# One-hots of an expert routing matrix made per token with tensor_scalar, and three rows of U h beside each block

## The chip, the cores and the metric

One core of a Trainium2 chip runs the whole kernel in one launch. The metric is the device time of an execution in microseconds; before the change three runs gave 2013.26, 2014.86 and 2017.14 us, a median of 2014.86.

## The reference

One layer over 512 latent tokens and 256 context tokens, width 1024: an input projection, two mixers (neighbourhood attention and a recurrence), an output projection, and then the part that matters here, an expert layer with 16384 experts. For each token, 8 heads score 128 + 128 sub-keys, take the best 16 of each side, add all pairs, and keep the best 16 sums. Each kept pair names an expert (i, j):

```
idx = take_along_axis(i1 * 128 + i2, pos)         # 8 heads x 16 experts per token
g   = softmax(top)
a   = gelu(einsum('tpkd,td->tpk', u[idx], t))
out = einsum('tpk,tpkd->td', g * a, v[idx])
```

A gated residual and a final RMSNorm follow.

## The kernel before, in words

The kernel does not gather the experts of the first 384 tokens. It computes the activations of all 16384 experts for these tokens as dense products, and multiplies them by a matrix W that holds the gate weight of each (expert, token) and is zero where the expert was not chosen. Only the last 128 tokens gather their rows of u and v by indirect DMA (`gathered`). Both ways run together.

The expert layer (`experts`) has these stages:

- Retrieval: queries, scores, and the search for the best 16 (`Retrieval.run`, `rank`). Beside it, `steps(RSTEPS)` issues three rows of U h after each of seven heads. One row (`Activations.step`) is 128 experts against 384 tokens: a load of u, a split into a rounded part (ScalarE, uhi) and a rest (GpSimd, ulo, line 69), 24 products of 384 columns (lines 396, 397, 399), and a gelu (line 400). The first seven pairs of rows stay in SBUF, later ones are written to DRAM and read back in the V stage.
- Routing: for each group of 128 tokens `slots` turns the expert numbers into two halves, transposes them on TensorE and copies them to eT (the two halves) and gw (the gate weight as a high and a low f16 part). Then twelve blocks of 32 tokens (`Routing.block`) build W. For one token, W is a 128 x 128 matrix: the product of the one-hot matrix of the second half (128 slots on the partitions, 128 values) with the one-hot matrix of the first half times the gate. VectorE makes four tokens at a time with two tensor_tensor operations (lines 348 and 351), laid out so that the token is the innermost index; TensorE does two products per token (line 356), ScalarE evicts four tokens (line 357), and one DMA per block writes 2 MB of W. Ahead of each block, `steps(WSTEPS)` issues two rows of U h.
- V stage: 128 iterations c, each with 18 products of 512 columns of a row of V against W times the activations (line 555). Rows of U h that are still missing are issued here, one per iteration, as soon as `up.n < c + 16`. The gathers of the last 128 tokens are issued between: per group of four iterations nine of them, or three while the rows of U h are ahead (`GRATE`, line 527). There are 259 gather iterations (128 rows of u, 128 of v, and a lag of 3); what is left after the loop runs behind it (line 567). Then `finish` normalises and writes the output.

The order of instructions on each engine is made by the framework's planner from the program order and its own estimates of durations, so rows of U h are interleaved with routing products; gathers and the operations on their rows are pinned to program order. Buffers (three hot, three hg, two stage, three uhi and ulo) bound how far an engine runs ahead. W must be in DRAM before the V stage's first loads.

Of the kernel before, what the change touches and what calls it, by code (L numbers as in the profile page):

```python
# [22 lines left out]
F32 = mybir.dt.float32  # L23
F32R = mybir.dt.float32r
F16 = mybir.dt.float16
U32 = mybir.dt.uint32
I32 = mybir.dt.int32
AF = mybir.ActivationFunctionType
ALU = mybir.AluOpType
# [3 lines left out]
P = 128  # L33
# [10 lines left out]
PH, NK, TOPK = 8, 128, 16  # L44
# [50 lines left out]
def layer(ctx: ExitStack, tc: tile.TileContext, a: dict):  # L95
# [49 lines left out]
    output_projection(tc, a, ident, ones, modx, s2x, mix, h2, hg, xnat)  # L145
    right.close()
    experts(tc, ctx, a, dram, ident, modx, h2, hg, xnat)


# [7 lines left out]
GSCALE = 2.0 ** 14  # L157
# [3 lines left out]
TD = ND * P  # L161


class Retrieval:
# [3 lines left out]
    def __init__(self, tc, ctx, a):  # L168
        nc = self.nc = tc.nc
        self.tc, self.a = tc, a  # L170
        self.pool = lambda c, name, bufs, **kw: c.enter_context(tc.tile_pool(name=name, bufs=bufs, reuse_waits="tile", **kw))
        one = self.pool(ctx, "r1", 1)
        self.top = one.tile([P, NT, PH, TOPK], F32, name="top")
        self.ex = one.tile([P, NT, PH, TOPK], F32, name="ex")
# [132 lines left out]
    def slots(self, m, wk, ps, ident, eT, gw):  # L307


        nc = self.nc  # L310
        flat = lambda t: t[:, m].rearrange("p h k -> p (h k)")
        sl = slice(m * P, (m + 1) * P)
        eu, ru = (wk.tile([P, P], U32, name=n) for n in ("eu", "ru"))
        rc = wk.tile([P, 2, P], F32, name="rc")
        nc.vector.tensor_copy(out=eu, in_=flat(self.ex))
        t = ps.tile([P, 3, P], F32, name="et", bufs=1)
        for i, (op, imm) in enumerate(((ALU.logical_shift_right, 7), (ALU.bitwise_and, NK - 1))):
            nc.vector.tensor_scalar(out=ru, in0=eu, scalar1=imm, scalar2=None, op0=op)
            nc.vector.tensor_copy(out=rc[:, i], in_=ru)
            nc.tensor.transpose(out=t[:, i], in_=rc[:, i], identity=ident)  # L320
        nc.tensor.transpose(out=t[:, 2], in_=flat(self.top), identity=ident)
        nc.scalar.activation(out=eT[:, :, sl], in_=t[:, 0:2], func=AF.Copy)
        nc.scalar.activation(out=gw[:, 0, sl], in_=t[:, 2], func=AF.Copy, scale=GSCALE)
        nc.vector.scalar_tensor_tensor(out=gw[:, 1, sl], in0=t[:, 2], scalar=GSCALE, in1=gw[:, 0, sl], op0=ALU.mult, op1=ALU.subtract)


class Routing:

    NB = 4

    def __init__(self, tc, ctx, a, ps, eT, g, W):
        nc = self.nc = tc.nc
        pool = lambda name, bufs, **kw: ctx.enter_context(tc.tile_pool(name=name, bufs=bufs, reuse_waits="tile", **kw))
        self.wk, self.st, self.ps = pool("wwk", 3), pool("wst", 2), ps
        self.eT, self.g, self.W = eT, g, W
        raw = self.st.tile([P, NK, WBLK], F32, name="stage").rearrange("p i t -> p (i t)")[:, 0:NK]
        nc.scalar.dma_start(out=raw, in_=a["iota"])
        self.iota = self.wk.tile([P, NK, self.NB], F16, name="iota16", bufs=1)
        nc.vector.tensor_copy(out=self.iota, in_=raw[:, :, None].to_broadcast([P, NK, self.NB]))

    def block(self, b):
        nc, NB = self.nc, self.NB
        stage = self.st.tile([P, NK, WBLK], F32, name="stage")
        for g in range(WBLK // NB):
            at = b * WBLK + g * NB
            shape = [P, 2, NK, NB]
            hot = self.wk.tile(shape, F16, name="hot")
            nc.vector.tensor_tensor(out=hot, in0=self.iota[:, None].to_broadcast(shape),
                                    in1=self.eT[:, :, None, at:at + NB].to_broadcast(shape), op=ALU.is_equal)
            hg = self.wk.tile(shape, F16, name="hg")  # L350
            nc.vector.tensor_tensor(out=hg, in0=hot[:, 0:1].to_broadcast(shape),
                                    in1=self.g[:, :, None, at:at + NB].to_broadcast(shape), op=ALU.mult)
            o = self.ps.tile([P, NB, NK], F32, name="wo")
            for t in range(NB):
                for i in range(2):
                    nc.tensor.matmul(out=o[:, t], lhsT=hot[:, 1, :, t], rhs=hg[:, i, :, t], start=(i == 0), stop=(i == 1))  # L356
            nc.scalar.activation(out=stage[:, :, g * NB:(g + 1) * NB].rearrange("p i t -> p t i"), in_=o, func=AF.Copy,
                                 scale=1.0 / GSCALE)
        nc.sync.dma_start(out=self.W[:, :, b].rearrange("g j x -> j g x"), in_=stage.rearrange("j (g i) t -> j g (i t)", i=GRP))
# [92 lines left out]
LASTV = ((0, 0), (0, 8), (2, 0), (2, 8))  # L452
WQB = 8
AHEAD, UBUFS = 9, 3
RSTEPS, WSTEPS = 3, 2
GRATE = (9, 3)


def experts(tc, ctx, a, dram, ident, modx, h2, hg, xnat):
    nc = tc.nc  # L460
# [14 lines left out]
    def steps(n):  # L475
        for _ in range(n):
            up.step()

    with ExitStack() as c2:
        c2.enter_context(tc.using_default_side("right"))  # L480
        ret = Retrieval(tc, c2, a)
        ret.run(h2, lambda: steps(RSTEPS))
        for g in range(2):
            sl = hg[:, g * 512:(g + 1) * 512]
            t = ups.tile([P, 4, P], F32, name="ut")
            for k in range(4):
                nc.tensor.transpose(out=t[:, k], in_=sl[:, k * P:(k + 1) * P], identity=ident)
            nc.scalar.activation(out=sl, in_=t.rearrange("p k d -> p (k d)"), func=AF.Copy)
        one = pool(c2, "w1", 1)
        eT = one.tile([P, 2, TD], F16, name="eT")  # L490
        gw = one.tile([P, 2, TD], F16, name="gw")
        ps = pool(c2, "wps", 2, space=PSUM)
        rt = Routing(tc, c2, a, ps, eT, gw, W)
        ret.softmax(one)
        for m in range(ND):
            ret.slots(m, one, ps, ident, eT, gw)
        nc.vector.tensor_copy(out=idx, in_=ret.ex[:, ND].rearrange("p h k -> p (h k)"))
        nc.gpsimd.tensor_copy(out=weight, in_=ret.top[:, ND].rearrange("p h k -> p (h k)"))
        for b in range(TD // WBLK):
            steps(WSTEPS)  # L500
            rt.block(b)
        steps(up.n % 2)
# [4 lines left out]
    with ExitStack() as c2:  # L507
# [14 lines left out]
        for c in range(NK):  # L522
            g, i = divmod(c, GRP)
# [4 lines left out]
            if i % 2 == 0:  # L528
                q = c // 2
                up.fetch(q + AHEAD)  # L530
                raw = vp.tile([P, 2, D], F32, name="vraw")
# [18 lines left out]
            for m in range(ND):  # L550
                sl = slice(m * P, (m + 1) * P)
                for r, vh, vl in vs:
                    for x, y in ((wh, vh), (wh, vl), (wl, vh)):
                        for d in range(2):
                            nc.tensor.matmul(out=acc[m][:, d * 512:(d + 1) * 512], lhsT=x[:, r, sl], rhs=y[:, d * 512:(d + 1) * 512],  # L555
                                             start=(c == 0 and y is vh and x is wh),
                                             stop=(last and r == 1 and x is wl))
# [41 lines left out]
class Weights:  # L599
# [22 lines left out]
    def col(self, ct):  # L622
        pieces = self.pieces
        return lambda k: tuple(t[:, k % 2, ct * P:(ct + 1) * P] for t in pieces[k // 2])
# [604 lines left out]
```

## Time and profile before

| what | value |
|---|---|
| profiled execution | 2013.56 us |
| its span | 2011.8 us |
| median of three runs | 2014.86 us |
| TensorE busy | 1832.2 us, 91% |
| VectorE busy | 1443.1 us, 72% |
| GpSimd busy | 954.2 us, 47% |
| ScalarE busy | 760.7 us, 38% |

Busy time is the time in which an engine has an instruction in it; matmuls are pipelined, so their durations overlap and the distance between starts is what one costs. The profile names instructions by line and by the tiles that they write and read (`out<-in`), with partitions x elements and type. In the timeline several equal instructions in a row are merged: the duration then runs from the first start to the last end. "PEld" is the loading of weights on TensorE. The profiled execution's time is 1.8 us over its span.

### The profile page before, as it was taken

To read this page: it belongs to the slowest core of one execution; us is meant where nothing else is said; L and a number is where in the kernel's file an instruction comes from. 1 tells how busy PE (TensorE), PEld (TensorE's weight loads), DVE (VectorE), ACT (ScalarE), POOL (GpSimd) and SP (SyncE) were. 2 spreads that over 40 slices of the span, in tenths; PEclk is the share of its full clock that TensorE was granted. 3 is DMA by queue.
4 is the path that set the end of the run, shared out by engine and by line. 5 is a ranking of instruction groups with operands and counts; after the bars stand their busy time and mean duration, and the time that the engine had idled before them with its cause. 6 is when DMAs were issued, how large, how long until landed. Compare 5 with 4: busy or idle time off the path is not lost.

```text
span 2011.8 us, 25393 instructions
## 1 busy us (share of the span) xinstructions
PE 1832.2 (91%) x9501; PEld 1578.0 (78%) x9501; DVE 1443.1 (72%) x2407; ACT 760.7 (38%) x1074; POOL 954.2 (47%) x651
## 2 busy tenths in 40 slices
PE   8999996998899999789988999999999999999870
PEld 4787875776777888688886889999999898888650
DVE  6625385668646799988856677777767777777877
ACT  5322243444435333267653333333333333333311
POOL 2411013333015355622215557767676777677663
PEclk8999997999998999999998999999999999999985
DMA  7317531000134333257778878878787878787885
GB/s 273 100 48 249 190 108 44 9 17 9 48 126 157 109 111 121 86 164 213 225 231 326 335 277 288 304 277 301 269 305 283 299 282 297 279 301 274 333 277 193
DMA packets 140506, 409.11 MB, mean 203 GB/s; under 512 B 11488, under 2 KB 62048, under 8 KB 123488
## 3 DMA queue, kind: packets, MB, share of 16 engines
q1 hardware_dynamic: 93440, 244.20, 34.3%
q0 software_dynamic: 42336, 153.24, 21.9%
q10 hardware_dynamic: 4608, 10.06, 1.3%
q8 instruction: 74, 1.21, 0.2%
q14 instruction: 48, 0.39, 0.1%
HBM read 370.76 MB, written 36.70 MB: 203 GB/s over the span
## 4 chain that ended last, share of the span: by engine, by line
PE 56%; DVE 15%; DMA 14%; issue 9%; POOL 4%; ACT 2%; SPq 0%; POOLq 0%; DVEq 0%; ACTq 0%
PE acc L555 17%; DMA rows<-v,gidx 10%; PE ua L399 6%; PE ua L397 5%; PE ua L396 5%; PE wo L356 3%; PE pj L78 2%; PE pj L77 2%; PE G L817 2%; PE pj L76 2%; DVE gacc L434 2%; POOL rows L417 1%; PE G L881 1%; DVE qk L810 1%; PE qp L78 1%
## 5 line engine op out<-in xcount | busy, mean ns | idle before, releaser
L396 PE MATMUL ua<-h,uhi 128*128 128x384 f32 x1024 | 347.1, 339 | 0.9 <-ACT act L400 0.9
L397 PE MATMUL ua<-h,uhi 128*128 128x384 f32 x1024 | 345.2, 337 | 0.0
L69 POOL TENSOR_TENSOR ulo<-uraw,uhi 128x1024 fp32r<-128x1024 f32 x87 | 213.6, 2458 | 207.4 <-PE ua L399 82.3
L422 DVE CUSTOM_DVE_ANT_0 rows<-rows,hg 128x1024 f32<-128x1024 f32 x128 | 200.0, 1576 | 99.2 <-DMA rows<-u,gidx 99.2
L434 DVE SCALAR_TENSOR_TENSOR gacc<-rows,dots,gacc 128x1024 f32<-128x1024 f32 x127 | 202.4, 1594 | 95.3 <-DMA rows<-v,gidx 93.8
L555 PE MATMUL acc<-vhi,wh 128*128 128x512 f32 x768 | 240.8, 395 | 14.0 <-ACT vhi L66 14.0
L555 PE MATMUL acc<-vlo,wh 128*128 128x512 f32 x768 | 240.5, 394 | 13.7 <-DVE vlo L69 13.7
L66 ACT ACTIVATE uhi<-uraw 128x1024 fp32r<-128x1024 f32 x128 | 135.8, 1062 | 283.4 <-DMA uraw<-uT 168.1
L555 PE MATMUL acc<-vhi,wl 128*128 128x512 f32 x768 | 239.6, 393 | 0.0
L417 POOL DMA_INDIRECT rows<-u,gidx x128 | 200.2, 1564 | 73.2 <-DVE dots L422 51.5
L417 POOL DMA_INDIRECT rows<-v,gidx x128 | 193.7, 1514 | 84.1 <-DVE gacc L434 55.1
L535 POOL TENSOR_TENSOR w<-w,act 128x768 f32<-128x768 f32 x64 | 145.2, 2287 | 144.5 <-DMA w<-W 139.6
L399 PE MATMUL ua<-h,ulo 128*128 128x384 f32 x1024 | 204.7, 338 | 2.8 <-POOL ulo L69 2.8
L396 PEld LDWEIGHTS ua<-h,uhi 128*128 128x128 f32 x1024 | 193.8, 189 | 5.1 <-ACT act L400 1.5
L397 PEld LDWEIGHTS ua<-h,uhi 128*128 128x128 f32 x1024 | 193.5, 189 | 4.2
L66 ACT ACTIVATE vhi<-vraw 128x1024 fp32r<-128x1024 f32 x128 | 134.6, 1054 | 149.8 <-PE acc L555 132.4
L69 DVE TENSOR_TENSOR vlo<-vraw,vhi 128x1024 fp32r<-128x1024 f32 x128 | 170.2, 1332 | 28.6 <-ACT vhi L66 28.6
L555 PEld LDWEIGHTS acc<-vlo,wh 128*128 128x128 f32 x768 | 144.9, 190 | 49.1 <-DVE vlo L69 17.3
L399 PEld LDWEIGHTS ua<-h,ulo 128*128 128x128 f32 x1024 | 179.0, 188 | 5.1 <-POOL ulo L69 5.0
L555 PEld LDWEIGHTS acc<-vhi,wh 128*128 128x128 f32 x768 | 144.4, 189 | 39.4 <-ACT vhi L66 14.3
L555 PEld LDWEIGHTS acc<-vhi,wl 128*128 128x128 f32 x768 | 145.4, 189 | 31.5
L618 DVE TENSOR_TENSOR wlo<-raw,whi 128x1024 fp32r<-128x1024 f32 (+1 forms) x68 | 80.1, 1196 | 93.4 <-ACT whi L615 92.9
(339 smaller groups left out, 3359.1 us busy)
## 6 DMA issues: line engine op xcount, KB each, us to landing
uraw<-uT SPq DMA_DIRECT2D x64, 1024.0 KB
vraw<-vP SPq DMA_DIRECT2D x64, 1024.0 KB
W<-stage SPq DMA_DIRECT2D x12, 2048.0 KB
w<-W SPq DMA_DIRECT2D x32, 768.0 KB
raw<-w_in SPq DMA_DIRECT2D x32, 512.0 KB
sg<-wmB POOLq DMA_DIRECT2D x21, 512.0 KB
raw<-wq SPq DMA_DIRECT2D x32, 256.0 KB
act<-act ACTq DMA_DIRECT2D x16, 384.0 KB
```

The source lines that it names most:

```text
L66: nc.scalar.activation(out=hi, in_=src, func=AF.Copy)
L69: (lo_eng or nc.vector).tensor_tensor(out=lo, in0=src, in1=hi.bitcast(F32), op=ALU.subtract)
L78: nc.tensor.matmul(out=out, lhsT=ll, rhs=rh, start=False, stop=stop and k == n - 1)
L396: nc.tensor.matmul(out=o, lhsT=hi[:, k], rhs=hh[:, k], start=(k == 0), stop=False)
L397: nc.tensor.matmul(out=o, lhsT=hi[:, k], rhs=hl[:, k], start=False, stop=False)
L399: nc.tensor.matmul(out=o, lhsT=lo[:, k], rhs=hh[:, k], start=False, stop=(k == KT - 1))
L417: tc.keep_in_program_order(nc.gpsimd.indirect_dma_start(out=t[:], out_offset=None, in_=a[src], in_offset=bass.IndirectOffsetOnAxis(ap=idx[ ...
L422: tc.keep_in_program_order(nc.vector.tensor_tensor_reduce(out=t, in0=t, in1=h, op0=ALU.mult, op1=ALU.add, scale=1.0, scalar=0.0, accum_out ...
L434: tc.keep_in_program_order(nc.vector.scalar_tensor_tensor(out=acc, in0=t, scalar=dots[:, s:s + 1], in1=acc, op0=ALU.mult, op1=ALU.add))
L535: nc.gpsimd.tensor_tensor(out=wp, in0=wp, op=ALU.mult, in1=rows(up.done[q]))
L555: nc.tensor.matmul(out=acc[m][:, d * 512:(d + 1) * 512], lhsT=x[:, r, sl], rhs=y[:, d * 512:(d + 1) * 512], start=(c == 0 and y is vh and ...
L618: lo_eng.tensor_tensor(out=lo, in0=raw, in1=hi.bitcast(F32), op=ALU.subtract)
```

## The change

The one-hots are made token by token: one tensor_scalar compares the list 0..127 with the token's second half (a scalar on each partition), and two more compare it with the first half and multiply by the high or the low part of the gate. hot and hg then hold each token's 128 values side by side. [...] And WSTEPS goes from 2 to 3.

```diff
@@ Retrieval.slots
+        g16 = wk.tile([P, P], F16, name="g16")
...
-        nc.scalar.activation(out=gw[:, 0, sl], in_=t[:, 2], func=AF.Copy, scale=GSCALE)
+        nc.scalar.activation(out=g16, in_=t[:, 2], func=AF.Copy, scale=GSCALE)
+        nc.vector.tensor_copy(out=gw[:, 0, sl], in_=g16)
@@ Routing.__init__
-        self.iota = self.wk.tile([P, NK, self.NB], F16, name="iota16", bufs=1)
-        nc.vector.tensor_copy(out=self.iota, in_=raw[:, :, None].to_broadcast([P, NK, self.NB]))
+        self.iota = self.wk.tile([P, NK], F16, name="iota16", bufs=1)
+        nc.vector.tensor_copy(out=self.iota, in_=raw)
@@ Routing.block
-            shape = [P, 2, NK, NB]
-            hot = self.wk.tile(shape, F16, name="hot")
-            nc.vector.tensor_tensor(out=hot, in0=self.iota[:, None].to_broadcast(shape),
-                                    in1=self.eT[:, :, None, at:at + NB].to_broadcast(shape), op=ALU.is_equal)
-            hg = self.wk.tile(shape, F16, name="hg")
-            nc.vector.tensor_tensor(out=hg, in0=hot[:, 0:1].to_broadcast(shape),
-                                    in1=self.g[:, :, None, at:at + NB].to_broadcast(shape), op=ALU.mult)
+            hot = self.wk.tile([P, NB, NK], F16, name="hot")
+            hg = self.wk.tile([P, NB, 2, NK], F16, name="hg")
+            for t in range(NB):
+                col = lambda x, i: x[:, i, at + t:at + t + 1]
+                nc.vector.tensor_scalar(out=hot[:, t], in0=self.iota, scalar1=col(self.eT, 1), scalar2=None, op0=ALU.is_equal)
+                for i in range(2):
+                    nc.vector.tensor_scalar(out=hg[:, t, i], in0=self.iota, scalar1=col(self.eT, 0), scalar2=col(self.g, i),
+                                            op0=ALU.is_equal, op1=ALU.mult)
...
-                    nc.tensor.matmul(out=o[:, t], lhsT=hot[:, 1, :, t], rhs=hg[:, i, :, t], start=(i == 0), stop=(i == 1))
+                    nc.tensor.matmul(out=o[:, t], lhsT=hot[:, t], rhs=hg[:, t, i], start=(i == 0), stop=(i == 1))
@@
-RSTEPS, WSTEPS = 3, 2
+RSTEPS, WSTEPS = 3, 3
@@ experts
-        eT = one.tile([P, 2, TD], F16, name="eT")
-        gw = one.tile([P, 2, TD], F16, name="gw")
+        eT = one.tile([P, 2, TD], F32, name="eT")
+        gw = one.tile([P, 2, TD], F32, name="gw")
```

## Rows read from the trace of the kernel before

**Rows 1.** The page: busy time of each engine; granted clock in 40 slices.

```profile
PE 1832.2 (91%) x9501; PEld 1578.0 (78%) x9501; DVE 1443.1 (72%) x2407; ACT 760.7 (38%) x1074; POOL 954.2 (47%) x651
PEclk8999997999998999999998999999999999999985
```

**Rows 2.** Table of stretches: us, busy (instructions) per engine, clock, DMA share, GB/s.

```profile
860.60:1042.30 181.70, 174.85 (x1225) 160.64 (x1224) 152.48 (x204) 128.28 (x139) 43.86 (x17) 1.00 0.68 206
...
1066.50:1207.00 140.50, 140.50 (x617) 116.72 (x618) 98.63 (x100) 49.86 (x53) 79.01 (x45) 0.99 0.82 310
1207.00:1867.80 660.80, 657.98 (x3321) 595.77 (x3320) 495.92 (x443) 225.59 (x277) 472.74 (x261) 1.00 0.79 288
1867.80:1949.00 81.20, 67.52 (x278) 53.46 (x277) 63.52 (x49) 20.19 (x21) 52.08 (x34) 0.96 0.87 317
1949.00:1991.80 42.80, 2.64 (x12) 1.86 (x10) 28.66 (x23) 0.00 (x0) 23.61 (x20) 0.56 0.76 258
```

**Rows 3.** Groups, 860.6 to 1042.3: count, busy us, mean ns, idle before.

```profile
L357 ACT ACTIVATE stage<-wo 128x512 f32<-128x512 f32 x96 | 103.1, 1123 | 41.5 <-PE wo L356 41.3
L356 PE MATMUL wo<-hg,hot 128*128 128x128 f16 x768 | 102.7, 296 | 6.6 <-DVE hg L351 6.2
L348 DVE TENSOR_TENSOR hot<-iota,eT 128x1024 f16<-128x1024 f16 x96 | 84.2, 885 | 25.5 <-PE wo L356 24.9 <-ACT eT L322 0.4
L356 PEld LDWEIGHTS <-hot 128*128 128x128 f16 x768 | 81.7, 118 | 20.3 <-DVE hg L351 11.8 <-issue 5.1 <-DVE gw L324 0.2
L351 DVE TENSOR_TENSOR hg<-hot,gw 128x1024 f16<-128x1024 f16 x96 | 73.0, 798 | 0.0
...
L69 POOL TENSOR_TENSOR ulo<-uraw,uhi 128x1024 fp32r<-128x1024 f32 x17 | 43.9, 2580 | 129.6 <-PE ua L399 58.6 <-ACT stage L357 41.8 <-ACT uhi L66 20.1
...
L396 PEld LDWEIGHTS ua<-h,uhi 128*128 128x128 f32 x149 | 29.1, 195 | 0.1
L66 ACT ACTIVATE uhi<-uraw 128x1024 fp32r<-128x1024 f32 x19 | 20.4, 1074 | 10.3 <-PE ua L397 10.2
```

**Rows 4.** Gelus of U h rows ended before routing, and in it (line 400).

```profile
L400 ACT ACTIVATE act<-ua x27: 467/490/494, 639.9 to 855.9; 128x384 f32<-128x384 f32 x27
...
L400 ACT ACTIVATE act<-ua x19: 492/540/566, 867.3 to 1042.1; 128x384 f32<-128x384 f32 x19
```

**Rows 5.** TensorE timeline (start us, us) and line 219's durations.

```profile
1017.35 2.05 PE L356 MATMUL wo<-hg,hot 128*128 128x128 f16 x16 [0.21 <-DVE hg L351]
...
1019.41 0.34 PE L397 MATMUL ua<-h,uhi 128*128 128x384 f32 x1
1019.58 0.34 PE L396 MATMUL ua<-h,uhi 128*128 128x384 f32 x1
1019.76 0.35 PE L397 MATMUL ua<-h,uhi 128*128 128x384 f32 x1
...
536.12 0.61 PE L881 MATMUL G<-npT,vnac 128*128 128x128 f32 x4
...
L219 PE MATMUL sp<-keys,q x128: 270/275/377, 631.0 to 816.2; 128*128 128x128 f32 x128
```

**Rows 6.** VectorE tensor_tensor by line: count, minimum/median/maximum ns, first and last start.

```profile
L348 DVE TENSOR_TENSOR hot<-iota,eT x96: 676/686/2906, 860.6 to 1036.9; 128x1024 f16<-128x1024 f16 x96
L351 DVE TENSOR_TENSOR hg<-hot,gw x96: 676/684/2901, 861.5 to 1037.6; 128x1024 f16<-128x1024 f16 x96
L281 DVE TENSOR_TENSOR hot<-at_near,posf x16: 302/319/2430, 698.9 to 849.5; 128x320 f16<-128x320 f16 x16
L281 DVE TENSOR_TENSOR hot<-at_all,posf x16: 555/564/673, 699.3 to 849.7; 128x800 f16<-128x800 f16 x16
...
L305 DVE TENSOR_TENSOR top<-top,sm x1: 691/691/691, 855.6 to 855.6; 128x512 f32<-128x512 f32 x1
...
L585 DVE TENSOR_TENSOR tsq<-acc,gate x3: 1214/1214/1218, 1993.0 to 1997.8; 128x1024 f32<-128x1024 f32 x3
```

**Rows 7.** VectorE with scalars: durations by line, then timeline (start us, us).

```profile
L431 DVE TENSOR_SCALAR gacc<-rows,dots x1: 753/753/753, 1583.3 to 1583.3; 128x1024 f32<-128x1024 f32 x1
...
L872 DVE TENSOR_SCALAR np<-np,nz x32: 449/486/489, 325.0 to 549.6; 128x512 f32<-128x512 f32 x32
...
L752 DVE SCALAR_TENSOR_TENSOR state<-state,dec,G x4: 341/341/348, 355.6 to 356.3; 128x128 f32<-128x128 f32 x4
...
355.55 1.12 DVE L752 SCALAR_TENSOR_TENSOR state<-state,dec,G 128x128 f32<-128x128 f32 x4 [3.94 <-PE G L745]
...
419.48 0.49 DVE L872 TENSOR_SCALAR np<-np,nz 128x512 f32<-128x512 f32 x1
419.88 0.42 DVE L820 COPY_PREDICATED amat<-masks,G 128x256 f32<-128x256 uint32 x1
...
2001.49 0.21 DVE L593 TENSOR_SCALAR tt<-tt 128x1 f32<-128x1 f32 x2
2001.61 0.14 DVE L588 TENSOR_SCALAR tv<-tv 128x1 f32<-128x1 f32 x1
```

**Rows 8.** Timeline of GpSimd and VectorE at 856; durations of line 319.

```profile
856.12 2.35 POOL L69 TENSOR_TENSOR ulo<-uraw,uhi 128x1024 fp32r<-128x1024 f32 x1 [1.39 <-ACT uhi L66]
856.19 2.36 DVE L319 CAST rc<-ru 128x128 f32<-128x128 uint32 x1
...
L319 DVE CAST rc<-ru x6: 219/224/2361, 856.2 to 865.8; 128x128 f32<-128x128 uint32 x6
```

**Rows 9.** The gathered rows' additions behind 1949 (line 434).

```profile
L434 DVE SCALAR_TENSOR_TENSOR gacc<-rows,dots,gacc x23: 1283/1285/1348, 1948.1 to 1990.5; 128x1024 f32<-128x1024 f32 x23
```

## The prediction

> **What bounds the kernel now.** I read the busy shares and slices of the page first, then a table of stretches, then the groups, waits and instruction spacings inside the one stretch that the change touches, then the end of the kernel. TensorE is busy for 91% of the span and is granted most of its clock [rows 1], but its stages have different limits. [...]
>
> TensorE's terms in routing: sixteen token products run in 2.05 us, so one starts every (2.05 - 0.30)/15 = 0.117 us; 768 of them make 89.8 us [rows 5]. A row of U h (24 products of 384 columns, started every 0.1725 us [rows 5]) makes 4.14 us; 27 rows end before the stage and 19 in it [rows 4], so 78.7 us. Together 168.5, and 13.2 us of the stage is neither.
>
> **The change, part by part.**
>
> *Products.* Same 768, now with contiguous operands. Their cost lies between 0.117 us as now and a third of a 384-column product, 0.0575 us: 89.8 or 44.2 us. The nearest row is a 128-column f32 product with contiguous moving rows, (0.61 - 0.275)/3 = 0.112 us [rows 5]; f16 weights load in 0.118 us where f32 ones take 0.195 [rows 3], so f16 may do better. I take 0.09 us, 69 us; under the forecast it lies beneath VectorE and does not enter the sum.
>
> [...]
>
> *One-hots.* Removed: 96 + 96 tensor_tensor of 1024 f16. They occupy 84.2 + 73.0 = 157.2 us [rows 3], of which 96 x (0.686 + 0.684) = 131.5 is their own [rows 6] and 25.7 is waiting behind the 17 GpSimd subtractions of ulo, 1.5 us for each; the longest one-hot took 2.906, that is 2.22 us more than its own [rows 6]. Added: three tensor_scalar of 128 f16 per token, 1152 in all, with one or two scalars read per partition. No row has this form, so I build it from its parts.
> - Data: f32 tensor_tensor runs (1.214 - 0.691)/512 = 1.02 ns an element, f16 tensor_tensor (0.564 - 0.319)/480 = 0.51, f32 tensor_scalar (0.753 - 0.486)/512 = 0.52 [rows 6, 7]. If f16 halves a tensor_scalar as it halves a tensor_tensor, 128 elements cost 0.033 us; if not, 0.067.
> - Fixed: four instructions of 128 f32 elements with a per-partition scalar (L752) take 1.12 us, each 0.341, so one starts every 0.260 us; less 0.131 of data leaves 0.129. L872 (512 f32, such a scalar too) is followed 0.40 us later by the next instruction, less 0.266 leaves 0.134. Without such a scalar two one-element tensor_scalar start 0.07 apart (0.21 for both, 0.14 for one) [rows 7]. So the fetched scalar costs about 0.06 us that the next instruction does not hide.
> - Sum: 0.129 + 0.033 = 0.162 us, 1152 times, 186.6 us. Low end 0.07 + 0.033 = 0.103 (fetch hidden): 119 us. High end 0.260, as L752 stands: 300 us. I take 0.162, since L872 is the nearest row in kind (tensor_scalar, both sides in SBUF) and agrees with L752 on the fixed part.
>
> [...]
>
> *GpSimd's ulo.* A single-source instruction is held by it as well: a 128-element cast that takes 0.224 us took 2.36 beside a subtraction that began 0.07 us before it [rows 8]. So each subtraction in the stage holds VectorE for up to 2.22 us. There were 17; with one more row in each of 12 blocks there are 29. At 1.5 us each 44, at 2.2 us 64. Now that VectorE is seldom idle I take 64.
>
> *VectorE in routing:* 186.6 + 64 + 3 (the slots of the other two token groups, and the added copy of g16) + 2 (last product and eviction) = 255.6 us. TensorE needs 69 to 89.8 + 31 x 4.14 = 128.3 + 13.2 = 211 to 231 us and is hidden beneath it; ScalarE needs 103 us of evictions and 1.07 + 0.54 us a row [rows 3, 4], 153 in all. The hot and hg tiles have three buffers, so VectorE runs up to 12 tokens ahead, and products queue on TensorE in order behind whichever one-hot is late. The stage grows by 255.6 - 181.7 = 74 us.
>
> *Rows moved.* Twelve rows leave the V stage: 12 x 4.14 = 49.7 us of TensorE there. But the pace of gathers follows up.n: a group of four rows of V issues three while the rows of U h are ahead of it and nine while they are not. With up.n = 46 at the start the groups at c = 0 to 28 issue three: 8 x 3 + 24 x 9 = 240 of 259 iterations in the loop, 19 behind it. With 58 eleven groups do: 33 + 189 = 222, and 37 behind it. The tail runs one per (1990.5 - 1948.1)/22 = 1.93 us [rows 9], so it grows by 18 x 1.93 = 34.7 us. Net in the V stage: -15 us. The moved rows' transfers (6 loads of 1 MB through SP, 6 more pairs of act written through ScalarE's queue and read back) add 8.4 MB to a stage that moves 206 x 181.7 = 37.4 MB [rows 2] and gets longer: hidden. The 2.4 MB read back fall where the DMA share is 0.82; uncovered they would cost 2.4/0.31 = 8 us.
>
> **Sum.** +74 - 15 = +59 us. The profiled execution took 2013.56 us (span 2011.8); 2072.5. The median of the runs is 1.3 us above it: 2074.
>
> **Rivals.**
> 1. *The one-hots cost more.* The second scalar costs another 0.06 us (768 instructions, +46), or f16 does not halve the data time (1152 x 0.034 = +39): about 2115. For: no row has two scalars or f16 here. Against: both might be fetched together.
> 2. *TensorE stays the bound, products as slow as now.* VectorE under 231 us (the fixed part at about 0.10, or subtractions that hold it 1.5 us): 231 - 181.7 - 15 = +35, 2049. [...]
> 3. *Faster.* Products start every 0.0575 us: 44.2 + 128.3 + 13.2 = 186 us; +4 - 15 = -11, 2004. It decides on VectorE: it must be done in 186 us, so one instruction in (186 - 5 - 44)/1152 = 0.119 us, between the spacing without a fetched scalar (0.103) and the one with it (0.162). For: L593's 0.07. Against: L752 and L872. [...]
> 4. Between 2 and 3: quick products, one-hots at 0.13 us: VectorE 150 + 50 + 5 = 205; +23 - 15, 2023.
> [...]
>
> **Chances.** Forecast (2055 to 2095) 0.50; rival 1 0.17; rival 2 0.11; rival 3 0.13; rival 4 0.05; rival 5 0.04. The range reaches from just above rival 3 to just above rival 1. Under 0.2% a measurement of this kernel cannot be told from no change. Faster is rival 3 and a little of 4: 0.15; within 0.2% 0.05; slower 0.80.
>
> **What would show it.** Starts of back-to-back tensor_scalar 0.16 us apart, at 0.10 rivals 3 and 4, at 0.20 or more rival 1. VectorE busy for over 90% of a routing stage of some 255 us, TensorE waiting for hg, not VectorE for products; if the reverse, rival 2. Long tensor_scalar of about 2.4 us, one beside each ulo on GpSimd. Start to start of the token products: 0.117, 0.06 or between. Between the last product of the V stage and the last gather some 35 us more. A shorter routing stage, or single tensor_scalar not held by GpSimd, would make the prediction wrong; so would gathers that catch up before the tail.

## The result, and the profile after

The changed kernel takes 2124.14 us (median of 4 runs, 2117.80 to 2128.88) against 2015.36 us before (the three runs above and a fourth, 2015.87): ratio 1.0538, 95% interval 1.0505 to 1.0572. It is slower by some 109 us where 59 were forecast. That is 29 us above the forecast's 2055 to 2095, and some 9 us above rival 1's 2115, just above which the range was to end. The profiled execution took 2128.88 us, its span is 2126.7.

The page of the kernel after, the lines that answer to [rows 1]: TensorE's share fell to 88%, VectorE made 140 us more, and the granted clock has a dip in the slice from 1117 to 1170 us that was not there (a slice is 2126.7/40 = 53.2 us).

```profile
PE 1870.1 (88%) x9501; PEld 1532.1 (72%) x9501; DVE 1582.8 (74%) x3364; ACT 761.5 (36%) x1074; POOL 959.0 (45%) x657
PEclk9999998999889999899995899999999999999965
```

The table of stretches after, for the whole routing stage and its last three parts (columns as in [rows 2]). The stage lasts 301.5 us where it lasted 181.7, and VectorE is busy for 299.57 of them.

```profile
863.40:1164.90 301.50, 259.44 (x1548) 163.32 (x1548) 299.57 (x1166) 147.32 (x165) 69.85 (x29) 0.90 0.48 153
...
1085.00:1110.00 25.00, 23.96 (x160) 15.98 (x159) 25.00 (x115) 13.25 (x15) 2.55 (x1) 1.00 0.53 158
1110.00:1135.00 25.00, 19.72 (x83) 7.60 (x82) 25.00 (x126) 10.79 (x11) 0.00 (x0) 0.56 0.56 159
1135.00:1164.90 29.90, 24.10 (x98) 9.66 (x98) 29.90 (x143) 13.16 (x14) 0.00 (x0) 0.50 0.26 71
```

The groups of that stage after (columns as in [rows 3]). TensorE's products now wait for hg (31.5 us, 6.2 before), and VectorE waits for nothing: 0.0 and 0.1 us.

```profile
L354 DVE TENSOR_SCALAR hg<-iota,eT,gw 128x128 f16<-128x128 f16 x768 | 256.8, 415 | 0.0
L359 PE MATMUL wo<-hg,hot 128*128 128x128 f16 x768 | 171.3, 237 | 41.5 <-DVE hg L354 31.5
L352 DVE TENSOR_SCALAR hot<-iota,eT 128x128 f16<-128x128 f16 x384 | 133.9, 349 | 0.1
...
L69 POOL TENSOR_TENSOR ulo<-uraw,uhi 128x1024 fp32r<-128x1024 f32 x29 | 69.9, 2409 | 163.0 <-ACT stage L360 57.3 <-PE ua L402 55.0 <-ACT uhi L66 21.6
```

And the timeline of the kernel after in the middle of the stage, VectorE's tokens and one GpSimd subtraction (start us, us):

```profile
960.12 0.25 DVE L352 TENSOR_SCALAR hot<-iota,eT 128x128 f16<-128x128 f16 x1
960.28 0.54 DVE L354 TENSOR_SCALAR hg<-iota,eT,gw 128x128 f16<-128x128 f16 x2
960.72 0.25 DVE L352 TENSOR_SCALAR hot<-iota,eT 128x128 f16<-128x128 f16 x1
960.88 0.54 DVE L354 TENSOR_SCALAR hg<-iota,eT,gw 128x128 f16<-128x128 f16 x2
...
962.54 0.27 DVE L352 TENSOR_SCALAR hot<-iota,eT 128x128 f16<-128x128 f16 x1
962.70 2.42 POOL L69 TENSOR_TENSOR ulo<-uraw,uhi 128x1024 fp32r<-128x1024 f32 x1 [4.99 <-issue]
962.70 2.69 DVE L354 TENSOR_SCALAR hg<-iota,eT,gw 128x128 f16<-128x128 f16 x2
965.31 0.24 DVE L352 TENSOR_SCALAR hot<-iota,eT 128x128 f16<-128x128 f16 x1
...
966.08 0.53 DVE L354 TENSOR_SCALAR hg<-iota,eT,gw 128x128 f16<-128x128 f16 x2
```

A hot is followed after 0.16 us. A token takes (962.54 - 960.12)/4 = 0.605 us, so an hg takes (0.605 - 0.16)/2 = 0.2225 us, 0.0625 more than a hot. Two hg that met a subtraction took 2.69 us instead of 0.53. So the stage is 384 x 0.605 = 232.3 us, 29 holds, and little else.

Where the 114.9 us of span went: the stage begins 2.8 us later (863.4, 860.6 before), is 119.8 us longer, and what follows it is 7.7 us shorter. The rows on this last part are the gelus of rows of U h up to the last one, and the additions of gathered rows behind it. First before, then after:

```profile
L400 ACT ACTIVATE act<-ua x84: 468/488/529, 1029.6 to 1867.6; 128x384 f32<-128x384 f32 x84
...
L434 DVE SCALAR_TENSOR_TENSOR gacc<-rows,dots,gacc x51: 1272/1285/3041, 1868.8 to 1990.5; 128x1024 f32<-128x1024 f32 x51
```

```profile
L403 ACT ACTIVATE act<-ua x70: 467/490/494, 1336.9 to 1944.7; 128x384 f32<-128x384 f32 x70
...
L437 DVE SCALAR_TENSOR_TENSOR gacc<-rows,dots,gacc x70: 1271/1285/3042, 1943.8 to 2105.2; 128x1024 f32<-128x1024 f32 x70
```

From the end of routing to the last of these gelus it is 780 us where it was 825: 45 less. From there to the last addition it is 160 us where it was 123, with 70 additions where there were 51: some 37 more.

### The profile page after: what moved, and what is told of

It reads as the page before. It is cut to its first block, busy times and chain, and to the rows that moved or that the text cites. A ratio compares the mean times of both kernels' runs of the same rounds, so it can differ in the third digit from the quotient of the medians.

```text
span 2126.7 us, 26331 instructions
## 1 busy us (share of the span) xinstructions
PE 1870.1 (88%) x9501; PEld 1532.1 (72%) x9501; DVE 1582.8 (74%) x3364; ACT 761.5 (36%) x1074; POOL 959.0 (45%) x657
## 5 line engine op out<-in xcount | busy, mean ns | idle before, releaser
L399 PE MATMUL ua<-h,uhi 128*128 128x384 f32 x1024 | 361.1, 353 | 0.6 <-ACT act L403 0.6
L69 POOL TENSOR_TENSOR ulo<-uraw,uhi 128x1024 fp32r<-128x1024 f32 x93 | 225.3, 2425 | 299.4 <-PE ua L402 166.8
L400 PE MATMUL ua<-h,uhi 128*128 128x384 f32 x1024 | 360.1, 352 | 0.0
L437 DVE SCALAR_TENSOR_TENSOR gacc<-rows,dots,gacc 128x1024 f32<-128x1024 f32 x127 | 192.6, 1517 | 94.0 <-DMA rows<-v,gidx 92.7
L354 DVE TENSOR_SCALAR hg<-iota,eT,gw 128x128 f16<-128x128 f16 x768 | 256.8, 415 | 0.0
L420 POOL DMA_INDIRECT rows<-u,gidx x128 | 192.8, 1506 | 84.4 <-DVE dots L425 63.6
L402 PE MATMUL ua<-h,ulo 128*128 128x384 f32 x1024 | 223.6, 353 | 3.4 <-POOL ulo L69 3.3
L420 POOL DMA_INDIRECT rows<-v,gidx x128 | 186.5, 1457 | 86.7 <-DVE gacc L437 57.6
L538 POOL TENSOR_TENSOR w<-w,act 128x768 f32<-128x768 f32 x64 | 153.7, 2418 | 144.3 <-DMA w<-W 129.9
L399 PEld LDWEIGHTS ua<-h,uhi 128*128 128x128 f32 x1024 | 196.1, 192 | 21.1 <-issue 16.8
L359 PE MATMUL wo<-hg,hot 128*128 128x128 f16 x768 | 171.3, 237 | 41.5 <-DVE hg L354 31.5
L400 PEld LDWEIGHTS ua<-h,uhi 128*128 128x128 f32 x1024 | 196.1, 192 | 6.6 <-issue 2.3
L402 PEld LDWEIGHTS ua<-h,ulo 128*128 128x128 f32 x1024 | 181.0, 192 | 6.4 <-POOL ulo L69 5.5
```

Source lines behind the costliest of these rows:

```text
L69: (lo_eng or nc.vector).tensor_tensor(out=lo, in0=src, in1=hi.bitcast(F32), op=ALU.subtract)
L354: nc.vector.tensor_scalar(out=hg[:, t, i], in0=self.iota, scalar1=col(self.eT, 0), scalar2=col(self.g, i), op0=ALU.is_equal, op1=ALU.mult)
L359: nc.tensor.matmul(out=o[:, t], lhsT=hot[:, t], rhs=hg[:, t, i], start=(i == 0), stop=(i == 1))
L399: nc.tensor.matmul(out=o, lhsT=hi[:, k], rhs=hh[:, k], start=(k == 0), stop=False)
L400: nc.tensor.matmul(out=o, lhsT=hi[:, k], rhs=hl[:, k], start=False, stop=False)
L402: nc.tensor.matmul(out=o, lhsT=lo[:, k], rhs=hh[:, k], start=False, stop=(k == KT - 1))
```

## The experiments

Times are medians; ratios are against runs of the kernel before on the same chip (medians of 2011.8 to 2018.7 us there). Stages are read from each trace, from the first hot to the end of the last eviction.

**The rows alone taken back.**

```diff
-RSTEPS, WSTEPS = 3, 3
+RSTEPS, WSTEPS = 3, 2
```

> The one-hots per token without the third row (WSTEPS back to 2). Theory: the routing stage lasts as long as VectorE's work in it, 0.605 us a token (384 tokens, 232 us), 2.2 us for each of GpSimd's ulo subtractions, and 5 us. With 17 instead of 29 of them it is 232 + 37 + 5 = 274 us instead of 301.5, and the rows that go back to the V stage cost about 8 us there: 2124 - 27 + 8 = 2105 us. Rival, the rows themselves hold the stage on TensorE (4.14 us each): 2124 - 50 + 8 = 2082 us. Second rival, the rows were free in the stage: 2132 us.

2112.37 us, ratio 1.0473 (1.0418 to 1.0528). The stretch of its routing stage:

```profile
862.80:1137.50 274.70, 232.36 (x1260) 129.81 (x1259) 273.95 (x1166) 129.41 (x140) 40.48 (x17) 0.77 0.44 136
```

274.7 us against 274 expected, VectorE busy throughout. Twelve GpSimd subtractions fewer took 301.5 - 274.7 = 26.8 us, 2.23 us each, as one whole hold; TensorE's 50 us of rows do not show. So the one-hots alone make the kernel 4.7% slower. The third row adds 0.65% to it, which is hardly clear of the noise of these two ratios: 27 us of stage, of which the V stage gives part back. The whole is 7 us over the 2105 expected. Its last gelu and last addition, to be set beside those of the kernel after:

```profile
L403 ACT ACTIVATE act<-ua x82: 469/492/494, 1256.9 to 1964.8; 128x384 f32<-128x384 f32 x82
...
L437 DVE SCALAR_TENSOR_TENSOR gacc<-rows,dots,gacc x127: 1270/1284/3712, 1681.4 to 2087.8; 128x1024 f32<-128x1024 f32 x127
```

From the end of routing to the last gelu it is 827 us where the kernel after has 780, and from there to the last addition 123 where that has 160: the moved rows gain 47 us and lose 37, 10 in all.

**The rows alone added to the kernel before.**

```diff
-RSTEPS, WSTEPS = 3, 2
+RSTEPS, WSTEPS = 3, 3
```

> The kernel before with three rows per block and nothing else. Theory: there TensorE bounds the stage, so each of 12 rows costs its 4.14 us: stage 182 + 50 = 231 us, V stage 8 us shorter: 2015 + 50 - 8 = 2057 us. Rival, the rows fit into gaps of TensorE: 2015 - 8 = 2007 us.

2046.80 us, ratio 1.0159 (1.0114 to 1.0205). Its stage, two of its groups, and its last gelu and addition:

```profile
859.90:1089.10 229.20, 225.74 (x1513) 211.44 (x1512) 159.44 (x204) 147.32 (x163) 71.69 (x29) 0.99 0.64 201
...
L351 DVE TENSOR_TENSOR hg<-hot,gw 128x1024 f16<-128x1024 f16 x96 | 81.7, 889 | 0.0
L348 DVE TENSOR_TENSOR hot<-iota,eT 128x1024 f16<-128x1024 f16 x96 | 81.7, 860 | 64.8 <-PE wo L356 64.2 <-ACT eT L322 0.4
...
L400 ACT ACTIVATE act<-ua x79: 468/490/547, 1031.1 to 1860.0; 128x384 f32<-128x384 f32 x79
...
L434 DVE SCALAR_TENSOR_TENSOR gacc<-rows,dots,gacc x127: 1268/1284/3822, 1650.8 to 2015.7; 128x1024 f32<-128x1024 f32 x127
```

229.2 us for 231 expected: TensorE bounds the stage of before, and a row costs it its full 4 us. The whole is 10 us under the 2057 expected, because more came back behind the stage than the 8 us of the theory: 771 us to the last gelu where the kernel before has 825, then 156 where that has 123, so 54 gained, 33 lost, and 22 in all by the unrounded figures.

**One scalar fewer in hg.**

```diff
-                    nc.vector.tensor_scalar(out=hg[:, t, i], in0=self.iota, scalar1=col(self.eT, 0), scalar2=col(self.g, i),
+                    nc.vector.tensor_scalar(out=hg[:, t, i], in0=self.iota, scalar1=col(self.eT, 0), scalar2=1.0,
```

> The kernel after, with hg's second per-partition scalar replaced by the constant 1.0 (the gate weights are left out of W); both operations stay. Theory: the second fetched scalar is what makes an hg 0.22 us against 0.16 for a hot; hg falls to 0.16, VectorE loses 768 x 0.0625 = 48 us, the stage is 253 us: 2076 us. Rival, the multiplication itself costs it, or the write to hg: no change, 2124 us.

2075.51 us, ratio 1.0301 (1.0256 to 1.0347). Its timeline and its stage:

```profile
960.46 0.24 DVE L352 TENSOR_SCALAR hot<-iota,eT 128x128 f16<-128x128 f16 x1
960.62 0.41 DVE L354 TENSOR_SCALAR hg<-iota,eT 128x128 f16<-128x128 f16 x2
960.95 0.24 DVE L352 TENSOR_SCALAR hot<-iota,eT 128x128 f16<-128x128 f16 x1
...
857.20:1113.20 256.00, 222.04 (x1530) 156.23 (x1530) 254.45 (x1166) 146.14 (x163) 69.16 (x29) 1.00 0.57 178
```

A token takes 0.49 us, each of its three instructions 0.163, although an hg still compares and multiplies. So the second scalar read from memory, not the second operation, is the 0.06 us; it made 301.5 - 256.0 = 45.5 us of the stage.

**GpSimd's subtractions moved to VectorE.**

```diff
+        up.lo = [nc.vector]
         for b in range(TD // WBLK):
             steps(WSTEPS)
```

> The kernel after with the ulo subtractions of the routing stage on VectorE instead of GpSimd. Theory: each GpSimd subtraction holds VectorE for 2.2 us and each costs 1.15 us when VectorE makes it itself; 29 x 1.05 = 30 us less, 2094 us. Rival, GpSimd's work lies beside VectorE's at no cost: 29 x 1.15 = 33 us more, 2157 us.

2149.41 us, ratio 1.0657 (1.0612 to 1.0702). The theory's 2094 is far off; the rival's 2157 is near, but its reason does not hold, as VectorE's busy time shows. The stage and three groups:

```profile
870.50:1193.10 322.60, 241.51 (x1474) 169.92 (x1473) 272.42 (x1194) 143.34 (x160) 2.39 (x1) 0.81 0.44 138
...
L352 DVE TENSOR_SCALAR hot<-iota,eT 128x128 f16<-128x128 f16 x384 | 96.2, 251 | 50.0 <-PE wo L359 49.7
...
L399 PE MATMUL ua<-h,uhi 128*128 128x384 f32 x233 | 103.5, 444 | 56.3 <-ACT uhi L66 56.3
...
L66 ACT ACTIVATE uhi<-uraw 128x1024 fp32r<-128x1024 f32 x30 | 31.3, 1058 | 56.6 <-DVE hg L354 39.4 <-DVE hot L352 8.8 <-DMA uraw<-uT 8.4
```

VectorE's busy time fell by 27 us, nearly the 30 of the theory, so the holds were real. But VectorE now stands 50 us behind products: ScalarE's uhi waits for hg (39.4 us), TensorE for uhi (56.3 us), and the one-hots for TensorE. I read this as the price of putting the subtractions into one queue with the one-hots; no run separates it further.

**Contiguous products alone.** In the kernel before, the operands of line 356 are read side by side: both (the diff), the weights alone, the moving operand alone (either half of it).

```diff
-                    nc.tensor.matmul(out=o[:, t], lhsT=hot[:, 1, :, t], rhs=hg[:, i, :, t], start=(i == 0), stop=(i == 1))
+                    nc.tensor.matmul(out=o[:, t], lhsT=hot[:, 1].rearrange("p k t -> p (k t)")[:, t * P:(t + 1) * P], rhs=hg[:, i].rearrange("p k t -> p (k t)")[:, t * P:(t + 1) * P], start=(i == 0), stop=(i == 1))
```

> The kernel before, with its own one-hots, but the products read 128 values side by side from both tiles (so each product mixes four tokens; W is not the reference's). Theory: contiguous operands let a product start every 0.055 us instead of 0.117, TensorE needs 42 + 79 + 13 = 134 us, VectorE with its 157 us and some waiting becomes the bound: stage about 168 us, 2001 us. Rival, contiguity is worth nothing: 2015 us.

> As the run with both operands contiguous, but only the weights (hot) are read side by side. Theory M, the strided moving operand (hg) is what slows a product: spacing stays 0.117 us, 2015 us. Theory W, the strided weights are: 0.055 to 0.06 us and 2001 us.

> As the run with both operands contiguous, but only the moving operand (hg) is read side by side. Theory M: 0.055 to 0.06 us a product, 2001 us. Theory W: 0.117 us, 2015 us.

Both: 2006.83 us, ratio 0.9953 (0.9926 to 0.9981). Weights: 2014.81, 0.9986 (0.9951 to 1.0022). Moving operand: 2010.26, 0.9976 (0.9952 to 1.0000). Eight products in a row on TensorE in each, in that order:

```profile
948.23 0.62 PE L356 MATMUL wo<-hg,hot 128*128 128x128 f16 x8
```

```profile
949.89 1.09 PE L356 MATMUL wo<-hg,hot 128*128 128x128 f16 x8
```

```profile
951.87 0.64 PE L356 MATMUL wo<-hg,hot 128*128 128x128 f16 x8
```

With one product's 0.23, 0.29 and 0.23 us taken off and seven spacings left, that is 0.056, 0.114 and 0.059 us: the stride of the moving operand alone doubled the price of a product. Theory M holds for the price; its 2001 us was not reached. The stage only went from 181.7 to 175.5 (both) and 176.8 us (moving). TensorE is busy for 35 us less, but the clock granted to it is 0.92 where it was 1.00, VectorE has 151 us of work, ScalarE waits 14.6 us for stores of W, and GpSimd's subtractions take 72 us where they took 44. How these share the rest of the stage the run does not separate:

```profile
865.60:1041.10 175.50, 139.87 (x1225) 124.65 (x1223) 150.75 (x204) 121.27 (x139) 72.10 (x17) 0.92 0.69 213
...
L357 ACT ACTIVATE stage<-wo 128x512 f32<-128x512 f32 x96 | 97.8, 1127 | 44.0 <-PE wo L356 28.9 <-DMA W<-stage 14.6 <-ACT act L400 0.4
...
L69 POOL TENSOR_TENSOR ulo<-uraw,uhi 128x1024 fp32r<-128x1024 f32 x17 | 72.1, 4248 | 96.4 <-PE ua L399 41.0 <-ACT uhi L66 30.2 <-ACT stage L357 25.3
```

**Contiguous products without more instructions.** Each value is stored twice side by side, so that a broadcast operand still has innermost step 1.

```diff
-            hot = self.wk.tile(shape, F16, name="hot")
-            nc.vector.tensor_tensor(out=hot, in0=self.iota[:, None].to_broadcast(shape),
-                                    in1=self.eT[:, :, None, at:at + NB].to_broadcast(shape), op=ALU.is_equal)
+            shape = [P, NB * 2, NK // 2, 2]
+            pair = lambda x: x.rearrange("p (k d) -> p k d", d=2)
+            flat = lambda x: x[:, at:at + NB].rearrange("p t i d -> p (t i) d")[:, :, None, :].to_broadcast(shape)
+            hot = self.wk.tile([P, NB, 2, NK], F16, name="hot")
+            nc.vector.tensor_tensor(out=hot.rearrange("p t i (k d) -> p (t i) k d", d=2),
+                                    in0=pair(self.iota)[:, None].to_broadcast(shape), in1=flat(self.eT), op=ALU.is_equal)
...
-                    nc.tensor.matmul(out=o[:, t], lhsT=hot[:, 1, :, t], rhs=hg[:, i, :, t], start=(i == 0), stop=(i == 1))
+                    nc.tensor.matmul(out=o[:, t], lhsT=hot[:, t, 1], rhs=hg[:, t, i], start=(i == 0), stop=(i == 1))
...
+        eT = one.tile([P, TD, 2, 2], F16, name="eT")
+        gw = one.tile([P, TD, 2, 2], F16, name="gw")
```

> Contiguous products without per-token instructions: eT and gw stay f16 and hold each value twice side by side, so a tensor_tensor over four tokens can write hot and hg token by token while its innermost step is still 1; two rows per block. Theory: it runs at the rate of the tensor_tensor before (hot 0.61 us, two hg of 512 at 0.34, so 1.29 us per four tokens, 124 us, and 17 subtractions of up to 2.2 us): stage about 166 us, 2000 us. Rival, the repeated pairs cost the half-price rate of f16: hot 1.13, hg 0.60 each, 224 + 37 = 261 us, 2094 us.

2015.18 us, ratio 0.9994 (0.9968 to 1.0020). The form runs at the rate hoped for (one hot takes 0.68 us and two 1.28, so one starts every 0.60), yet the stage is 181.0 us where 166 were hoped for. Its first store of W and the load ahead of it on the SP queue, and GpSimd's long pair of subtractions, from the timeline; then the stretches around them:

```profile
864.30 34.12 SPq L395 DMA_DIRECT2D uraw<-uT  x2
898.47 9.06 SPq L366 DMA_DIRECT2D W<-stage  x2
```

```profile
881.65 19.16 POOL L69 TENSOR_TENSOR ulo<-uraw,uhi 128x1024 fp32r<-128x1024 f32 x2 [6.46 <-PE ua L406]
```

```profile
880.00:895.00 15.00, 14.94 (x140) 12.71 (x139) 15.00 (x36) 13.81 (x17) 13.35 (x1) 1.00 0.07 28
895.00:910.00 15.00, 2.54 (x25) 2.17 (x24) 9.82 (x8) 0.86 (x2) 8.29 (x3) 0.70 0.77 222
```

While VectorE has no gap, from 880 to 895, one GpSimd subtraction does not end; the next load of u waits for it (33.4 us in all), the first store of W waits behind that load, ScalarE for the store, and TensorE does 2.5 us of work between 895 and 910.

**The store on another queue.** In the kernel with pairs and in the kernel before:

```diff
-        nc.sync.dma_start(out=self.W[:, :, b].rearrange("g j x -> j g x"), in_=stage.rearrange("j (g i) t -> j g (i t)", i=GRP))
+        nc.scalar.dma_start(out=self.W[:, :, b].rearrange("g j x -> j g x"), in_=stage.rearrange("j (g i) t -> j g (i t)", i=GRP))
```

> The kernel with pairs (contiguous products, two tensor_tensor forms), whose block store of W goes through ScalarE's queue instead of SP's. In the run with pairs SP held the first store behind a load of u that waited 33 us for GpSimd, ScalarE then waited 20.8 us in all for stage buffers and TensorE stood for some 14 us. Theory, the queue order is what keeps that stage at 181 us: about 20 us less, 161 us and 1995 us. Rival, the store's own transfer time or VectorE's 160 us with its holds are the limit: 2012 to 2015 us.

> The kernel before with only that move of the store to ScalarE's queue. TensorE bounds its stage and ScalarE waited for no store there, so both theories expect no change: 2015 us, within 5.

With pairs 2015.25 us, ratio 0.9988 (0.9965 to 1.0011); from before 2037.00, 1.0107 (1.0078 to 1.0136). With pairs ScalarE's wait for the store, 20.8 us, is gone, and nothing is gained: the stage is 182.3 us, and what bounds it now stays open. The kernel before had no such wait to lose; it takes 22 us more, which neither theory expected. Its stage:

```profile
855.40:1063.80 208.40, 192.69 (x1273) 177.09 (x1272) 159.67 (x205) 127.26 (x141) 47.14 (x18) 0.90 0.61 188
```

It is 208.4 us, 27 longer, and TensorE runs 1273 products in it where it ran 1225 [rows 2]: the 48 of two rows of U h, 8 us, so the planner made another order. The granted clock is 0.90 where it was 1.00; how much of the other 19 us that is, and what came first, stays open.

**More gathers while the rows are ahead.** In the kernel after:

```diff
-GRATE = (9, 3)
+GRATE = (9, 5)
```

> The kernel after with five instead of three gathers per group of four while the rows of U h are ahead. Theory: the moved rows shorten the V stage by up to 50 us but eighteen more gathers are left for the tail at about 2.0 us; with 11 x 5 + 21 x 9 = 244 gathers in the loop 15 are left instead of 37, the tail is 44 us shorter, and the early groups, whose transfers grow from 5.0 to 6.0 MB in 16.8 us, lose some 20 us of it: 2124 - 24 = 2100 us. Rival, transfers are the limit all along and a gather costs the same wherever it stands: 2124 us.

2112.05 us, ratio 1.0475 (1.0438 to 1.0513), 12 us less than the kernel after where 24 were expected; the two intervals just touch. Its last gelu and last addition:

```profile
L403 ACT ACTIVATE act<-ua x80: 470/488/539, 1031.2 to 1973.4; 128x384 f32<-128x384 f32 x80
...
L437 DVE SCALAR_TENSOR_TENSOR gacc<-rows,dots,gacc x127: 1270/1285/4065, 1680.7 to 2090.2; 128x1024 f32<-128x1024 f32 x127
```

From the last gelu of U h to the last addition it is 117 us instead of 160, some 43 less for 44 expected; from the end of routing (1164.3) to that gelu 809 instead of 780, 29 more for some 20. So the tail is set by how many gathers are left, and much of what it gives is lost earlier. That the transfers take it there is the theory; the run does not show it.

**One instruction less for hg.** The kernel with pairs, hg over all four tokens and both parts in one tensor_tensor of 1024.

```diff
+            both = [P, NB, 2, NK // 2, 2]
+            nc.vector.tensor_tensor(out=hg.rearrange("p t i (k d) -> p t i k d", d=2),
+                                    in0=hot[:, :, 0].rearrange("p t (k d) -> p t k d", d=2)[:, :, None].to_broadcast(both),
+                                    in1=self.g[:, at:at + NB][:, :, :, None, :].to_broadcast(both), op=ALU.mult)
```

> The kernel with pairs (store on SP's queue again, two rows per block), hg made by one tensor_tensor of 1024 instead of two of 512. Theory, with contiguous products VectorE and the holds by GpSimd set its stage: one instruction less per four tokens takes 96 x 0.10 = 10 us from VectorE, so 171 us of stage and 2005 us, faster than both kernels. Rival, the waits of the planned order (loads of u and stores of W in one queue, GpSimd held off by VectorE) set it: 181 us and 2015 us.

2000.53 us, ratio 0.9943 (0.9920 to 0.9966): 0.6% faster than the kernel before. Its stage and ScalarE's evictions:

```profile
858.20:1025.60 167.40, 139.93 (x1224) 125.70 (x1223) 153.83 (x201) 122.01 (x141) 77.00 (x17) 0.94 0.73 223
...
L363 ACT ACTIVATE stage<-wo 128x512 f32<-128x512 f32 x96 | 98.1, 1130 | 36.2 <-PE wo L362 34.7 <-DMA W<-stage 1.0 <-ACT act L406 0.4
```

It is 14.3 us shorter than before and 13.6 shorter than with pairs alone, with VectorE busy for 153.83 of 167.4. This does not decide between the theory and its rival: VectorE's busy time fell by 5.6 us (159.45 with pairs), and at the same time ScalarE's wait for stores of W went from 20.8 us to 1.0.

## Why the prediction was wrong in size and right in kind

- *That VectorE would take over as the bound, at 0.16 us an instruction:* it took over from TensorE, which was busy for 174.85 us of the 181.7 before [rows 2]: VectorE is busy for 299.57 of 301.5 us; the price is right for the one-hots with one scalar. The fixed 0.129 us from L752 and the halved f16 data time [rows 6, 7] gave 0.162; the trace has 0.16.
- *"Sum: 0.129 + 0.033 = 0.162 us, 1152 times, 186.6 us":* this step failed. It priced hot and hg alike, although 768 of the 1152 read two scalars. They cost 0.2225 us, so the one-hots make 232.3 us, 45.7 more than forecast. That is the first form of rival 1, which had 0.17 and said about 2115; its second form, f16 data at full price, is ruled out by the 0.16. The run with one scalar fewer gives back 45.5 us and has the stage of the forecast, 256.0 us. The rows of before held no instruction with two such scalars, so the size could not be read there; but the prediction had itself put one fetched scalar at about 0.06 us [rows 7], and took the second as free without a row that let it.
- *GpSimd's hold, 29 x 2.2 = 64 us:* right; 2.23 us each from the run with two rows. The trace of the kernel after agrees, with 2.69 us instead of 0.53 for two hg beside a subtraction of 2.42.
- *Stage 255.6 us:* measured 301.5, and the difference, 45.9, is the second scalar: 45.5 by the run with one scalar fewer.
- *TensorE hidden, products between 0.0575 and 0.117 us:* hidden, yes; my middle of 0.09 us was too dear, contiguous ones started 0.056 us apart. It was the moving operand whose stride of 8 bytes in f16 doubled the price of a product here (0.114 us against 0.056). The weights bore that stride (0.059 us against 0.056).
- *Rows moved, -15 us:* about right, and so was the reason. Between the kernel before and the kernel after it is -8: the rows gave 45 of the 49.7 us, and eighteen more gathers took back 37, for 34.7. Between kernels that differ by the third row alone it is -10 (the kernel after against the run with two rows) and -22 (the run with three rows against the kernel before), so the 7 us by which it missed lie within what these pairs differ by.
- *Sum:* +59 forecast, +115 in the profiled execution: 46 from the second scalar, 7 from the V stage, 3 from the later start of the stage. The last two are no finding: the stage began anywhere from 855.4 to 870.5 us in the runs here.

## What to carry to other kernels

Price an instruction by its spacing behind others of its kind, and count what it reads: the second scalar fetched from memory was 0.06 us here, twice the 0.03 us that I estimate for the data of a 128-element instruction. Twelve instructions over 128 elements took 4 x 0.605 = 2.42 us where two over 1024 took 1.37 [rows 6], and even at 0.16 us each they would take 1.92. When an operation must be reshaped for the engine behind it, first look for a layout in which the large instruction still works (values stored in pairs), and find out which of the two operands needs it. Here the pairs alone gained nothing, and 0.6% with one instruction fewer. And here the stage that lost its bound found the next one close by: 35 us less work on TensorE were worth 6 us of stage.

## What the runs showed that I had not expected

- The second scalar's price, 0.2225 - 0.16 = 0.06 us, is as large as the first's, which is an estimate: 0.07 us between one-element tensor_scalar with constants [rows 7] and 0.033 of data make 0.10, and with one fetched scalar it is 0.16.
- With a moving operand of 128 f16 at a stride of 8 bytes a product started every 0.114 us, with a contiguous one every 0.056 to 0.059; the weights' stride cost 0.003 us of that.
- GpSimd and VectorE held each other off unequally here. Beside the many short tensor_scalar a subtraction still took 2.41 us in the mean; beside tensor_tensor of 512 and 1024 elements with no gaps between them it took up to 16.4 (4.25 in the mean of the stage in the run with both operands contiguous), as the durations of ulo in the run with pairs show (minimum/median/maximum ns):

```profile
L69 POOL TENSOR_TENSOR ulo<-uraw,uhi x87: 2337/2407/16413, 637.7 to 1854.1; 128x1024 fp32r<-128x1024 f32 x87
```

- The products of U h stopped at 1108 us in the kernel after, so for the next 55 us TensorE ran token products alone, two every 0.61 us. Its granted clock was 0.56 in the mean from 1110 to 1135, and 0.50 from there to the end of the stage. It cost nothing there, since VectorE was busy throughout (25.00 of 25.00 us, then 29.90 of 29.90).
